# Sliding attention with 640-column key tiles and one 256-column product pair for every query tile

## Chip, cores and metric

The kernel runs on one core of one Trainium2 chip, as one launch. The metric is the device time of an execution in microseconds. Before the change the median of 3 runs is 2957.75 us (2957.2 to 2959.73).

## The reference, cut to what matters

Two transformer blocks over 2048 tokens of width 1024. The part that the change touches is the second block's mixer: causal attention in a window of 128 keys, 16 query heads in 4 groups, 4 key and value heads (one per group), head width 64, a bias by distance and a sink per head.

```python
def banded_attention(q, k, v, t5_table, window, sinks=None):
    ...
    kb = jnp.concatenate([kp[:, :, j:j + nb] for j in range(nprev + 1)], axis=3)
    ...
    s = jnp.einsum('bgrnqd,bgnkd->bgrnqk', qb, kb) * (Dh ** -0.5)
    ...
    s = jnp.where(valid, s + bias[None, :, :, None], NEG)
    ...
    o = jnp.einsum('bgrnqk,bgnkd->bgrnqd', p.astype(v.dtype), vb)
```

A tile of 128 queries needs 256 keys: its own 128 and the 128 in front of them. `xn @ w_in` gives q, k, v and a gate z; the output is `(o * silu(z)) @ w_out`, added to the residual and normalised.

## The kernel before, in words

`kernel_body` runs stages one after the other: projections of the first block (`phase_a`), its two attentions (`phase_b1`, `phase_b2`), its output and gate (`phase_c`), the sliding attention with its projections (`phase_d`), and the last product (`phase_e`). Every value that goes into a product is kept as a high and a low half, so a projection is three products for each k (`mm3`, lines 803 to 806). Tensors pass between stages through DRAM.

`phase_c` ends, for each tile t of 128 tokens, with `part3(t)` (lines 916 to 927): it scales the row tile `c_xt` by the norm and by `c_ng` (line 922), transposes it in eight 128-column pieces (line 839, out `c_tp`), and stores both halves to `s_xt`, 512 tokens to a tensor. `part2(15)` and `part3(15)` are the last work of the stage.

`phase_d` takes the tokens in 4 blocks of 512. `load_x` (line 1015) loads eight `e_x` tiles of 512 KB for a block from `s_xt`; each projection (q, z, v, k; output in `e_mm`, three PSUM buffers) walks over k = 0 to 7 of them. `kproj` writes four pairs of key tiles `kst` of 512 columns (`e_k`, one pair per group, high and low); before it writes a block's keys it copies the last 128 columns of the block before to `kpv` (`e_kp`, line 1061, on POOL). `scores(n)` handles step n = 16·block + 4·group + j, one tile of 128 queries and one group: for each of 4 heads it makes 128x256 scores in `e_s`. For j > 0 that is one pair of products with 256 columns (high and low key half, line 1106). For j = 0 the keys lie in two tiles, and it is a pair with 128 columns on `kpv` (line 1110) and another on `kst` (line 1112). DVE adds the bias and takes the maximum (line 1114), ACT the exponential, POOL the scaling; `values(n)` follows two steps later: eight transposes (line 1141), the split on ACT and DVE (lines 1145, 1146), four products of 512 columns (lines 1150, 1151), the sum on DVE (line 1158), the gate on POOL and a store. The projections of the next group or block are dealt out between the steps as pieces (lines 1164 to 1201).

`phase_e` (lines 1207 to 1270) loads and splits the weights into `f_w`, and for each tile t splits `f_yr` into `f_y` (ACT line 1239, then POOL line 1240), runs 48 products (`f_mm`), adds the tile `f_xt` (line 1252 loads it) and normalises.

The order of instructions on each engine and on SP's queue is made at build time by a planner, which takes what is ready by its own simulation, in program order among the ready ones; on the chip each queue then runs in that order.

**Where tiles lie.** A stage's pools are stacked in the order in which they are opened, from the same start, in bytes per partition; the next stage's pools are laid over them once the stage is closed. A pool of the next stage that lies over an old pool waits for the old one. Worked out from the tile shapes, the pools that matter are:

| stage c | bytes | stage d | bytes | stage e | bytes |
|---|---|---|---|---|---|
| c_a (`c_at`) | 40960 to 65536 | e_p | 64512 to 76800 | f_x1 (7 `f_xt`) | 53248 to 81920 |
| c_x (3 `c_xt`) | 65536 to 77824 | e_kv (`e_kp`) | 76800 to 80896 | f_s | 81920 to 83200 |
| c_wo1 (weights) | 77824 to 110592 | e_s | 80896 to 81664 | f_w1 | 83200 to 115968 |
| c_y1 | 110592 to 114688 | e_a0 (8 `e_x`) | 81664 to 114432 | f_y (2 `f_y`) | 115968 to 132352 |
| c_t, c_s | 114688 to 124352 | e_a1 (5 `e_x`) | 114432 to 134912 | f_j | 132352 to 134400 |
| c_w (`c_wg`, `c_wj`, `c_ng`) | from 124352 | e_q (8 `e_q`) | 134912 to 151296 | f_x2 (2 `f_xt`) | 134400 to 142592 |
| | | e_z, e_v | 151296 to 175872 | | |
| | | e_k (`e_k`) | 175872 to 192256 | | |

The 13 `e_x` buffers are used in turn: block 0 has the eight of e_a0, block 1 starts with the five of e_a1, and block 3 has its k = 0 and 1 in e_a1 and k = 2 to 7 in e_a0.

Of the kernel before, what the change touches and what calls it, by code (L numbers as in the profile page):

```python
# [7 lines left out]
F32 = mybir.dt.float32  # L8
F32R = mybir.dt.float32r
# [7 lines left out]
P = 128  # L17
# [963 lines left out]
def phase_d(tc, c, scr, a_w_in):  # L981
    nc = tc.nc
# [3 lines left out]
    with (  # L986
# [3 lines left out]
        tc.tile_pool(name="e_b", bufs=2) as bp,  # L990
        tc.tile_pool(name="e_t", bufs=2) as tp,
        tc.tile_pool(name="e_p", bufs=3) as pp,
        tc.tile_pool(name="e_kv", bufs=1) as kvp,
        tc.tile_pool(name="e_s", bufs=6) as sp,
        tc.tile_pool(name="e_a0", bufs=8) as ap0,
        tc.tile_pool(name="e_a1", bufs=5) as ap1,
# [8 lines left out]
        tc.tile_pool(name="e_po", bufs=1, space=PSUM) as ps_o,  # L1005
    ):
        toep = scr["toep"].rearrange("h r u -> h (r u)")[:, 127:127 + P * 383].rearrange("h (p w) -> p h w", w=383)
        kst = [[kp.tile([P, 512], F32R, name=f"e_k{g}{i}") for i in range(2)] for g in range(4)]
        kpv = [[kvp.tile([P, P], F32R, name=f"e_kp{g}{i}") for i in range(2)] for g in range(4)]
        vts, xts, qs, zs, units, bias, st = {}, {}, {}, {}, {}, {}, {}  # L1010

        def load_x(blk):
# [17 lines left out]
        def tmode(blk, key, m):  # L1030
            ps = pm.tile([P, 512], F32, name="e_mm")
            ms = slice(m * P, (m + 1) * P)
            for k in range(KD):
                w = units[key][k // 4]
                x = xts[blk, k]
                mm3(nc, ps, w[:, 0, k % 4, ms], w[:, 1, k % 4, ms], x[:, 0], x[:, 1], k == 0, k == KD - 1)
            return ps
# [17 lines left out]
        def kproj(blk, m):  # L1055
            ps = tmode(blk, ("k", blk), m)
            for e in range(2):
                g = 2 * m + e
                if blk > 0:
                    for i in range(2):  # L1060
                        nc.gpsimd.tensor_scalar(kpv[g][i], kst[g][i][:, 384:512].bitcast(F32), 1.0, 1.0,
                                                ALU.mult, ALU.mult)
                src = ps[64 * e:64 * e + 64]
                kh, kl = kst[g]
                for half in range(2):
                    hs = slice(64 * half, 64 * half + 64)
                    nc.scalar.activation(kh[hs], src, AF.Copy)
                    nc.vector.tensor_sub(kl[hs], src, kh[hs].bitcast(F32))  # L1068
# [15 lines left out]
        def scores(n):  # L1084
            blk, g, j = n // 16, (n // 4) % 4, n % 4
            t = blk * BT + j
            first = t == 0
            c0 = 128 if first else 0
            qsl = slice(j * P, (j + 1) * P)
            if j == 0:  # L1090
                b = bp.tile([P, 4, 256], F32, name="e_bias")
                nc.sync.dma_start(b, toep[:, 4 * g:4 * g + 4, 0:256])
                bias[blk, g] = b
            b = bias[blk, g]
            es = ep.tile([P, 4, 256], F32, name="e_es")
            mx = sp.tile([P, 4], F32, name="e_mx")
            ll = sp.tile([P, 4], F32, name="e_l")
            kk = kst[g]
            for r in range(4):
                if r % 2 == 0:  # L1100
                    ps2 = ps_s.tile([P, 2, 256], F32, name="e_s")
                ps = ps2[:, r % 2]
                q = qs[blk, g, r]
                if j > 0:
                    for i in range(2):
                        nc.tensor.matmul(ps, q[:, qsl], kk[i][:, (j - 1) * P:(j + 1) * P], start=i == 0, stop=i == 1)  # L1106
                else:
                    if not first:
                        for i in range(2):
                            nc.tensor.matmul(ps[:, 0:P], q[:, qsl], kpv[g][i], start=i == 0, stop=i == 1)  # L1110
                    for i in range(2):
                        nc.tensor.matmul(ps[:, P:256], q[:, qsl], kk[i][:, 0:P], start=i == 0, stop=i == 1)
                hd = 4 * g + r
                nc.vector.tensor_tensor_reduce(es[:, r, c0:], ps[:, c0:], b[:, r, c0:], 1.0, sk8[:, hd:hd + 1],  # L1114
                                               ALU.add, ALU.max, mx[:, r:r + 1])
            nm = sp.tile([P, 4], F32, name="e_nm")
            nc.vector.tensor_scalar(nm, mx, -0.125, None, ALU.mult)
            for r in range(4):
                nc.scalar.activation(es[:, r, c0:], es[:, r, c0:], AF.Exp, bias=nm[:, r:r + 1], scale=0.125,
                                     accum_out=ll[:, r:r + 1])  # L1120
            sk = sp.tile([P, 4], F32, name="e_sk4")
            nc.vector.tensor_sub(sk, sk8[:, 4 * g:4 * g + 4], mx)
            nc.scalar.activation(sk, sk, AF.Exp, scale=0.125)
            nc.vector.tensor_add(ll, ll, sk)
            nc.vector.reciprocal(ll, ll)  # L1125
            for r in range(4):
                nc.gpsimd.tensor_scalar(es[:, r, c0:], es[:, r, c0:], ll[:, r:r + 1], 0.5, ALU.mult, ALU.mult)  # L1127
            st[n] = es
# [43 lines left out]
        def block_pieces(blk):  # L1172
            yield lambda: load_x(blk)
            yield from group_pieces(blk, 0)
            yield lambda: load_unit(("v", blk), 1280)
            for j in range(BT):
                yield lambda j=j: vproj(blk, j)
            yield lambda: load_unit(("k", blk), 1024)
            for m in range(2):
                yield lambda m=m: kproj(blk, m)  # L1180
# [6 lines left out]
        for n in range(N + LAG):  # L1187
            blk, g, j = n // 16, (n // 4) % 4, n % 4
            if n < N and j == 0:
                nxt = group_pieces(blk, g + 1) if g < 3 else block_pieces(blk + 1) if blk + 1 < NB else iter(())  # L1190
                pend = list(nxt)
                per = -(-len(pend) // 4)
            if n < N:
                scores(n)
            for f in pend[:per // 2]:
                f()
            if n >= LAG:
                values(n - LAG)
            for f in pend[per // 2:per]:
                f()  # L1200
            pend = pend[per:]
# [126 lines left out]
def kernel_body(tc, a, out):  # L1328
    with (
        tc.tile_pool(name="const", bufs=1) as cp,  # L1330
        tc.tile_pool(name="dram", bufs=1, space=DRAM) as dp,
    ):
        c = consts(tc, cp)
        scr = make_scratch(dp)
        phase_a(tc, c, a["x"], a["w_in"], a["mix_norm_g"],
                [a["diff_q_norm_g"], a["diff_k_norm_g"], a["dil_q_norm_g"], a["dil_k_norm_g"]], scr,
                lambda pm: [
                    diff_lambda(tc, c, [a["lambda_q1"], a["lambda_k1"], a["lambda_q2"], a["lambda_k2"]]),
                    prep_swa(tc, c, scr, a["t5_table_2"], a["t_onehot"], a["a_sinks_2"], pm)])
        phase_b1(tc, c, scr, a["t_ndist"], a["diff_sub_norm_g"], c["lam"])  # L1340
        phase_b2(tc, c, scr, a["t_nat"], a["t_res"], a["t_two"])
        phase_c(tc, c, scr, a["x"], a["p"], a["w_out"], a["ple_norm_g"], a["w_ple_gate"], a["w_ple_proj"],
                a["norm_g_2"])
        phase_d(tc, c, scr, a["a_w_in_2"])
        phase_e(tc, c, scr, a["a_w_out_2"], a["final_g_2"], out)
# [29 lines left out]
```

## Time and profile before

| | |
|---|---|
| median of 3 runs | 2957.75 us |
| the profiled execution | 2958.66 us |
| its span in the trace | 2956.9 us |
| instructions | 45164 |
| PE, weight loads, DVE, ACT, POOL busy | 97%, 83%, 61%, 53%, 42% |

The profiled execution is 0.91 us above the median, and 1.76 us of it lie around the span. In rows of instructions the first number is the start in us from the span's start, the second the time that the row covers, then the engine (PEld is the weight load, SPq the DMA issue on SP), the line, the operation, out<-in, the shape and the count. A matmul's own duration contains its way through the array, so that what it costs in a stream is read from the distance of the starts.

### The profile page before, as it was taken

The numbers are of one execution on the slowest core, as the hardware profiler recorded it, in microseconds if no ns is written. First come the engines' busy times: TensorE is split into PE (matmuls) and PEld (weight loads), VectorE is DVE, ScalarE is ACT, GpSimd is POOL, SyncE is SP. The second block draws the span as 40 slices with busy tenths as digits, with TensorE's granted clock in tenths as the row PEclk, the third lists the DMA queues.
The fourth block names the chain that finished last, engine by engine and source line by source line (L and its number), as shares of the span: only waits on it lengthen the run. The fifth ranks groups of instructions, "written<-read, shape, count | busy, mean of one in ns | idle before, by whom it ended". The sixth has DMA issues, their size and how long they took to land.

```text
span 2956.9 us, 45164 instructions
## 1 busy us (share of the span) xinstructions
PE 2878.8 (97%) x15554; PEld 2455.2 (83%) x15554; DVE 1803.7 (61%) x4607; ACT 1562.5 (53%) x3480; POOL 1239.1 (42%) x1156
## 2 busy tenths in 40 slices
PE   9999999999999999989999899999999999999998
PEld 7878888888798888878999778888788888888787
DVE  4215556522688888887877654444535756666855
ACT  5222333221588888878989442222345756665621
POOL 1110111001488888864777700000156555555421
PEclk9999999999999999999999899999999999999999
DMA  6663444424314132129786633232554243332552
GB/s 208 116 160 86 122 114 121 96 87 115 121 30 115 46 106 65 51 64 189 143 164 133 180 116 110 77 113 92 183 166 155 86 157 96 109 100 72 156 182 79
DMA packets 410646, 346.00 MB, mean 117 GB/s; under 512 B 89745, under 2 KB 356401, under 8 KB 408497
## 3 DMA queue, kind: packets, MB, share of 16 engines
q1 hardware_dynamic: 388000, 329.24, 40.2%
q10 hardware_dynamic: 20736, 8.65, 1.8%
q0 software_dynamic: 1680, 5.21, 0.7%
q8 instruction: 124, 2.03, 0.3%
q14 instruction: 106, 0.86, 0.1%
HBM read 227.51 MB, written 116.52 MB: 116 GB/s over the span
## 4 chain that ended last, share of the span: by engine, by line
PE 86%; DMA 5%; DVE 3%; ACT 2%; SPq 1%; issue 1%; POOL 0%; DVEq 0%; ACTq 0%; POOLq 0%
PE s_ps L331 8%; PE psm L190 7%; PE psm L192 7%; PE psm L191 7%; PE e_mm L804 5%; PE e_mm L806 5%; PE e_mm L805 5%; PE c_mm L804 4%; PE c_mm L805 4%; PE c_mm L806 4%; PE t_ps L375 3%; PE o_ps L389 2%; PE o_ps L391 2%; PE o_ps L390 2%; PE d_sr L590 2%; PE f_mm L805 2%
## 5 line engine op out<-in xcount | busy, mean ns | idle before, releaser
L190 PE MATMUL psm<-w,hh 128*128 128x512 f32 x1024 | 406.3, 398 | 9.4 <-DVE t L111 8.0
L191 PE MATMUL psm<-w,hl 128*128 128x512 f32 x1024 | 399.5, 391 | 0.0
L192 PE MATMUL psm<-w,hh 128*128 128x512 f32 x1024 | 399.5, 393 | 0.0
L101 POOL TENSOR_TENSOR w<-wraw,w 128x512 fp32r<-128x512 f32 x64 | 81.5, 1294 | 600.2 <-ACT w L100 589.9
L365 POOL TENSOR_TENSOR et<-et 128x1024 f32<-128x1024 f32 x124 | 296.0, 2409 | 0.0
L331 PE MATMUL s_ps<-kst,qst 128*128 128x512 f32 x1024 | 289.7, 407 | 5.5 <-DVE mx L337 3.7
L347 ACT ACTIVATE et<-et,nm 128x2048 f32<-128x2048 f32 x128 | 257.2, 2009 | 5.2
L1026 POOL TENSOR_TENSOR e_wt<-e_raw,e_wt 128x1024 fp32r<-128x1024 f32 x80 | 191.3, 2399 | 111.9 <-ACT e_wt L1025 110.9
L190 PEld LDWEIGHTS psm<-w,hh 128*128 128x128 f32 x1024 | 193.5, 189 | 48.3 <-DVE t L111 8.4
L804 PE MATMUL e_mm<-e_x,e_wt 128*128 128x512 f32 x576 | 228.2, 396 | 1.2 <-DVE e_k L1068 0.8
L806 PE MATMUL e_mm<-e_x,e_wt 128*128 128x512 f32 x576 | 226.8, 394 | 0.0
L192 PEld LDWEIGHTS psm<-w,hh 128*128 128x128 f32 x1024 | 192.9, 189 | 40.9
L805 PE MATMUL e_mm<-e_x,e_wt 128*128 128x512 f32 x576 | 226.6, 393 | 0.0
L191 PEld LDWEIGHTS psm<-w,hl 128*128 128x128 f32 x1024 | 193.7, 189 | 38.2
L331 PEld LDWEIGHTS s_ps<-kst,qst 128*128 128x128 f32 x1024 | 175.9, 190 | 45.3 <-DVE mx L337 18.1
L1127 POOL TENSOR_SCALAR e_es<-e_es,e_l 128x256 f32<-128x256 f32 (+1 forms) x256 | 119.4, 485 | 170.8 <-DVE e_l L1125 118.6
L364 POOL TENSOR_SCALAR et<-et,cc 128x1024 f32<-128x1024 f32 x124 | 138.2, 1129 | 110.3 <-PE psm L192 57.1
L377 DVE TENSOR_TENSOR ptl<-t_ps,pth 128x512 fp32r<-128x512 f32 x256 | 169.4, 684 | 19.9 <-ACT pth L376 16.8
L337 DVE CUSTOM_DVE_ANT_0 et<-s_ps,nd,mx 128x1024 f32<-128x1024 f32 x128 | 163.9, 1280 | 26.5 <-PE s_ps L331 24.7
L1114 DVE CUSTOM_DVE_ANT_0 e_es<-e_s,e_bias,e_sk 128x256 f32<-128x256 f32 (+1 forms) x256 | 117.4, 473 | 102.6 <-PE e_s L1106 71.2
L376 ACT ACTIVATE pth<-t_ps 128x512 fp32r<-128x512 f32 x256 | 143.6, 595 | 44.8 <-PE t_ps L375 41.1
L850 POOL TENSOR_TENSOR c_yn<-c_yn,ssq_sub 128x512 f32<-128x512 f32 x16 | 17.0, 1061 | 354.1 <-DMA c_yn<-s_y 354.1
(268 smaller groups left out, 7848.2 us busy)
## 6 DMA issues: line engine op xcount, KB each, us to landing
e_raw<-in_a_w_in_dram SPq DMA_DIRECT2D x80, 512.0 KB, 3.7
wraw<-in_w_in_dram SPq DMA_DIRECT2D x64, 256.0 KB, 3.5
kst<-s_dk SPq DMA_DIRECT2D x128, 128.0 KB, 4.2
s_xt<-c_at SPq DMA_DIRECT2D x32, 512.0 KB, 6.8
e_x<-s_xt SPq DMA_DIRECT2D x32, 512.0 KB, 7.1
t<-in_x_dram SPq DMA_DIRECT2D x32, 256.0 KB, 5.4
s_dv<-t SPq DMA_DIRECT2D x32, 256.0 KB, 3.3
s_bv<-t SPq DMA_DIRECT2D x32, 256.0 KB, 3.6
```

The source lines that it names most:

```text
L190: nc.tensor.matmul(ps, ah, cur[k][:, 0], start=k == 0, stop=False)
L191: nc.tensor.matmul(ps, al, cur[k][:, 0], start=False, stop=False)
L192: nc.tensor.matmul(ps, ah, cur[k][:, 1], start=False, stop=k == KD - 1)
L331: nc.tensor.matmul(ps[:, b * 512:b * 512 + 512], lhs, heads[h, "k", e, i, 2 * hf + b], start=i == 0, stop=i == 1)
L337: nc.vector.tensor_tensor_reduce(et[:, hf], ps, bias[:, off:off + 1024], 1.0, -3.0e38 if hf == 0 else mx[:, 0:1], ALU.add, ALU.max, mx[:, ...
L347: nc.scalar.activation(ev, ev, AF.Exp, bias=nm, scale=slope, accum_out=st[g]["l"][:, e:e + 1])
L365: nc.gpsimd.tensor_sub(es[0][:, hf], es[0][:, hf], es[1][:, hf])
L377: nc.vector.tensor_sub(tl[:, :, qi], pt, th[:, :, qi].bitcast(F32))
L804: nc.tensor.matmul(ps, ah, bh, start=first, stop=False)
L805: nc.tensor.matmul(ps, al, bh, start=False, stop=False)
L806: nc.tensor.matmul(ps, ah, bl, start=False, stop=last)
L1026: nc.gpsimd.tensor_sub(w[:, 1], raw, w[:, 0].bitcast(F32))
```

## The change

The pool e_kv with the `e_kp` tiles goes. The key tiles have 640 columns: 128 for the keys in front of the block, then the block's 512. The POOL copy goes into the first 128 columns of the same tile, and every query tile is scored by one pair of products with 256 columns (128 for the first tile of all). The instruction count falls by 96 products with their weight loads. In the stack of stage d the pools e_s to e_v begin 4096 bytes earlier (e_s at 76800, e_a0 at 77568, e_a1 at 110336, e_q at 130816), e_k begins at 171776 and ends at 192256 as before.

```diff
-        tc.tile_pool(name="e_kv", bufs=1) as kvp,
...
-        kst = [[kp.tile([P, 512], F32R, name=f"e_k{g}{i}") for i in range(2)] for g in range(4)]
-        kpv = [[kvp.tile([P, P], F32R, name=f"e_kp{g}{i}") for i in range(2)] for g in range(4)]
+        kst = [[kp.tile([P, P + 512], F32R, name=f"e_k{g}{i}") for i in range(2)] for g in range(4)]
...
-                        nc.gpsimd.tensor_scalar(kpv[g][i], kst[g][i][:, 384:512].bitcast(F32), 1.0, 1.0,
+                        nc.gpsimd.tensor_scalar(kst[g][i][:, 0:P], kst[g][i][:, 512:].bitcast(F32), 1.0, 1.0,
                                                 ALU.mult, ALU.mult)
...
-                kh, kl = kst[g]
+                kh, kl = [k[:, P:] for k in kst[g]]
...
-                if j > 0:
-                    for i in range(2):
-                        nc.tensor.matmul(ps, q[:, qsl], kk[i][:, (j - 1) * P:(j + 1) * P], start=i == 0, stop=i == 1)
-                else:
-                    if not first:
-                        for i in range(2):
-                            nc.tensor.matmul(ps[:, 0:P], q[:, qsl], kpv[g][i], start=i == 0, stop=i == 1)
-                    for i in range(2):
-                        nc.tensor.matmul(ps[:, P:256], q[:, qsl], kk[i][:, 0:P], start=i == 0, stop=i == 1)
+                for i in range(2):
+                    nc.tensor.matmul(ps[:, c0:], q[:, qsl], kk[i][:, j * P + c0:(j + 2) * P], start=i == 0, stop=i == 1)
```

## Rows read from the trace of the kernel before

**Rows 1.** The page, busy time of each engine over the span.
```profile
PE 2878.8 (97%) x15554; PEld 2455.2 (83%) x15554; DVE 1803.7 (61%) x4607; ACT 1562.5 (53%) x3480; POOL 1239.1 (42%) x1156
```

**Rows 2.** Busy time by stretch: one block of stage d.
```profile
core 0: us, PE busy (x) PEld busy (x) DVE busy (x) ACT busy (x) POOL busy (x), PEclk, DMA share, GB/s
2335.00:2491.00 156.00, 156.00 (x868) 134.71 (x867) 96.22 (x287) 98.63 (x247) 92.76 (x125) 1.00 0.39 122
```

**Rows 3.** The instructions of line 1110: min/median/max ns, first and last start.
```profile
L1110 PE MATMUL e_s<-e_kp,e_q x96: 220/274/307, 2332.4 to 2762.6; 128*128 128x128 f32 x96
```

**Rows 4.** PE in order of time, 2728.3 to 2730.2: one head at j = 0.
```profile
2728.30 0.40 PE L804 MATMUL e_mm<-e_x,e_wt 128*128 128x512 f32 x1
...
2728.99 0.33 PE L1110 MATMUL e_s<-e_kp,e_q 128*128 128x128 f32 x2
2729.16 0.39 PE L1112 MATMUL e_s<-e_k,e_q 128*128 128x128 f32 x2
...
2730.13 0.39 PE L804 MATMUL e_mm<-e_x,e_wt 128*128 128x512 f32 x1
```

**Rows 5.** PE in order of time, 2737.8 to 2739.5: one head at j > 0.
```profile
2737.85 0.40 PE L804 MATMUL e_mm<-e_x,e_wt 128*128 128x512 f32 x1
...
2738.55 0.40 PE L1106 MATMUL e_s<-e_k,e_q 128*128 128x256 f32 x2
...
2739.48 0.39 PE L804 MATMUL e_mm<-e_x,e_wt 128*128 128x512 f32 x1
```

**Rows 6.** All engines at 2106: c_wo's last product, block 0's first load.
```profile
2105.99 0.40 PE L806 MATMUL c_mm<-c_wo,c_at 128*128 128x512 f32 x1
...
2106.42 0.34 SPq L1015 DMA_DIRECT2D e_x<-s_xt  x1
```

**Rows 7.** DVE, then SP's queue, at 2144: c_ng's last use, block 1's loads.
```profile
2143.11 1.28 DVE L922 SCALAR_TENSOR_TENSOR c_xt<-c_xt,rd_y,c_ng 128x1024 f32<-128x1024 f32 x1
...
2144.53 3.37 SPq L1015 DMA_DIRECT2D e_x<-s_xt  x5
```

**Rows 8.** All engines at 2791: the last scores, two loads of f_xt.
```profile
2790.91 0.40 PE L1106 MATMUL e_s<-e_k,e_q 128*128 128x256 f32 x2
...
2791.68 0.95 SPq L1252 DMA_DIRECT2D f_xt<-s_x  x2
```

**Rows 9.** PE at 2138: transposes of part3(14), first projection of stage d.
```profile
2137.86 1.03 PE L839 MATMUL c_tp<-id,c_xt 128*128 128x128 f32 x8
2138.87 0.50 PE L804 MATMUL e_mm<-e_x,e_wt 128*128 128x512 f32 x1
```

**Rows 10.** Line 1015 in 2144 to 2148: issues, and issue to landing.
```profile
L1015 SPq DMA_DIRECT2D e_x<-s_xt x5: 332/443/1539, 2144.5 to 2147.5; - x5
...
DMA to landing us min/median/max: 4.7/6.4/7.2
```

**Rows 11.** PE idle before 2750.20, and by stretch the 4.8 us behind it.
```profile
2750.20 0.91 PE L1106 MATMUL e_s<-e_k,e_q 128*128 128x256 f32 x4 [2.76 <-DVE e_mx L1114]
...
2750.20:2755.00 4.80, 4.75 (x21) 3.90 (x21) 4.73 (x18) 4.75 (x17) 2.12 (x5) 0.64 0.81 263
```

**Rows 12.** By stretch, 2755.66 to 2791.30: all instructions, then those of f_mm alone.
```profile
2755.66:2791.30 35.64, 34.85 (x183) 28.59 (x183) 29.04 (x85) 25.76 (x66) 19.69 (x32) 1.00 0.38 110
...
2755.66:2791.30 35.64, 25.50 (x96) 17.11 (x96) 1.51 (x3) 1.00 0.38 110
```

**Rows 13.** Groups by line in the same stretch: DVE's work for the steps.
```profile
L1114 DVE CUSTOM_DVE_ANT_0 e_es<-e_s,e_bias,e_sk 128x256 f32<-128x256 f32 x16 | 7.4, 475 | 0.4 <-PE e_s L1106 0.3
...
L1146 DVE TENSOR_TENSOR e_pl<-e_tp,e_ph 128x512 fp32r<-128x512 f32 x10 | 6.6, 684 | 0.1
...
L1158 DVE TENSOR_TENSOR e_o<-e_o,e_tmpb 64x256 f32<-64x256 f32 x10 | 4.1, 415 | 1.2 <-ACT e_tmpb L1153 1.1
```

**Rows 14.** Who writes f_y: min/median/max ns, first and last start.
```profile
L1239 ACT ACTIVATE f_y<-f_yr x16: 1043/1062/1064, 2745.7 to 2926.8; 128x1024 fp32r<-128x1024 f32 x16
L1240 POOL TENSOR_TENSOR f_y<-f_yr,f_y x16: 2354/2394/2402, 2746.8 to 2928.0; 128x1024 fp32r<-128x1024 f32 x16
```

## The prediction

> **What bounds the kernel now.** I read the page first: PE is busy for 97% of the span, and apart from its own weight loads nothing for more than 61% [rows 1]. Then the stage: in the block from 2335 to 2491 us PE is busy for all 156.00 us [rows 2], so there every product taken from PE shortens the kernel by what it costs in the stream. Then the two kinds of scores in the order of time [rows 4, 5], for that cost. Last the two seams, from `phase_c` to `phase_d` and from there to `phase_e`, since the change also moves pools, and a PE without work is paid in full where PE is the bound.
>
> **The saving: 8.8 us.** 96 instructions of line 1110 [rows 3] are two for each of 48 heads at j = 0 (3 blocks, 4 groups, 4 heads); each such head has two on line 1112 too, and makes two of 256 columns instead of four of 128. In [rows 4] 1.83 us pass from 2728.30 to 2730.13, with six products of 512 columns besides the four narrow ones (three before and three behind); in [rows 5] 1.63 us pass with six such products and the wide pair. The difference, 0.20 us, is a head's saving: 48 x 0.20 = 9.6 us. The last four heads (step 60) lie in the tail, where PE will not be the bound (below): 44 x 0.20 = 8.8 us. In parts: a 512-column product takes 0.23 us (2737.85 to 2738.55 holds three), so the wide pair costs 1.63 - 1.38 = 0.25 us and the four narrow ones 0.45, 0.11 each against 0.125. The Trainium skill (TensorE: Matmul & The Clock Gate, Back-to-back issue gap) lists for an isolated product 134 cycles at 128 columns and 262 at 256, warm; by that four narrow ones would cost as much as two wide ones and the saving would be nil. The measured rows decide.
>
> **The copy: nothing.** Same size, same engine, two for each group and block. It is now a write to the tile that the next block's keys are written to; those writes wait for the last scores of the group anyway. If the copy too waits for all scores on that tile, POOL stands a little longer, and `e_k` is late by a copy: under 1 us a block at worst, so 0 to 3 us. I take 0, PE having other projections there.
>
> **The first seam: e_a0 now lies over c_x, 15 us.** Pools wait whole. Block 0's first `e_x` load is issued at 2106.42, as the last product on `c_wo` (2105.99) ends [rows 6], though its own bytes lie under the weights of k = 0 and 1. Block 1's loads go at 2144.53, just after line 922 has read `c_ng` for the last time (2144.39), though `c_ng` lies behind their own bytes: they share a pool's edge, not bytes [rows 7]. The third case is at the other seam: `f_xt` for t = 2 goes 0.4 us after the last scores, the last reader of `e_q` [rows 8]. With e_a0 at 77568 and c_x up to 77824, 256 bytes overlap, and block 0's eight loads wait no longer for the weights but for the last `c_xt`, that of `part3(15)`. Line 922 ends at 2144.39, its eight transposes take 1.03 us [rows 9], so the loads go at about 2145.4 instead of 2106.42. PE has no other work: today it starts the projections at 2138.87 [rows 9], and all of them need block 0's `e_x`.
>
> How long: from issue to landing takes 4.7 us for the first tile, and the five of block 1, issued in 3.0 us, land 1.3 us apart [rows 10]. If block 0's go first, x of k = 0 lands at 2150.1, PE idles from 2138.9 less the 1.03 of transposes that it has to do anyway: 10 us. If block 1's five (ready 1 us earlier, with SP idle) go first, 5 x 1.3 us come on top: 16 us. I take 13, about half of them in front. Behind it, one projection wants a tile every 0.69 us (three products) and gets one every 1.3 us: 7 x 0.6 = 4 us, or 0 where the two others with a free PSUM buffer run beside it; I take 0, as the planner takes what is ready. And the clock: after PE had been idle for 2.76 us, the granted clock was 0.64 over the next 4.8 us [rows 11], between its levels of 2.4 and 1.2 GHz; that costs 4.8 x 0.36 = 1.7 us. Together 15 us, from 10 to 22.
>
> **The second seam: f_y now lies over e_q, 11 us.** f_y ends at 132352; e_q began at 134912 and now begins at 130816. Today `f_y` is first written at 2745.7 [rows 14], and tiles 0 and 1 of `phase_e` fill PE while the last steps 60 to 63 wait for DVE, ACT and POOL: 96 products of `f_mm`, 96 x 0.23 = 22 us of the 35.64 us up to the last scores [rows 12]. After the change `f_y` waits for the last scores. So the last steps run alone. How fast: DVE has for them 4 x 4 x 0.475 us for the scores and 3 x (2 x 0.684 + 2 x 0.415) us for the values in front, 7.6 + 6.6 = 14 us if nothing else ran on it; with all that it does in this stretch it is busy for 29 us [rows 12, 13]. I take 20 us, nearer to the first, since the steps come first in program order; the weight splits of `phase_e` stay and share DVE and ACT. Then ACT's 1.06 us before the first `f_mm`, and 2.39 us on POOL before the first product with the low half [rows 14], which the remaining values partly cover. In these 21 us PE does 15 heads x 0.25 us and four steps of values at 8 x 0.11 + 4 x 0.23 = 1.8 us: 11 us; idle are 10, and with the slower clock 1 more. Bounds: 14 us of steps with three values leave 14 + 1 - 9 = 6 us; 29 us leave 30 - 11 = 19.
>
> **The sum.** -8.8 + 15 + 11 = +17.2 us against the profiled execution's 2958.66, so 2975.9; the median lies 0.9 lower: **2975.0 us**. Bounds: -8.8 + 10 + 6 = +7, and -8.8 + 22 + 19 + 3 = +35.
>
> **Rivals.**
> *Faster: the pools' shift costs nothing.* Either a load waits only for tiles still in use under its own bytes (seven of block 0's eight then wait for nothing new, and the projections can start on what is there), or the planner finds an order that hides both waits. Then the saving stands alone: 2957.75 - 9.6 = 2948.1 us. It decides at the point where the first load of block 0 goes before about 2134 (4.7 us ahead of 2138.87). Against it stand three places where the whole pool is waited for [rows 6 to 8]. Chance 0.09.
> *Only the first seam:* the tail is long enough on other engines that `f_mm` is not missed, or `f_y` comes early. 2957.75 - 8.8 + 15 = 2964. Chance 0.12.
> *Only the second:* block 0's loads are not held. 2957.75 - 8.8 + 11 = 2960, no change that can be told. Chance 0.06.
> *Narrow products are not dear.* If a product cost by its columns alone, with 0.23 us for 512, four of 128 would cost as much as two of 256 and nothing would be saved: 2957.75 + 26 = 2984. The skill's list above would have it so. Rows 4 and 5 speak against it; chance 0.03.
> That the products are the same sums, only joined, is plain from the diff; no rival there.
>
> **How the numbers follow.** A measurement of this kernel tells 0.2%, 5.9 us, from no change: from 2951.8 to 2963.7. The forecast has 0.70. Slower is the forecast, narrow products, and half of the first-seam case, whose time is at the edge: 0.70 + 0.03 + 0.06 = 0.79. Same is the other half and the second-seam case, 0.12; faster is the first rival, 0.09. The range goes from 2959, which takes in either seam alone, to 2986, +28, short of the upper bound +35, which needs every cost at its worst; it leaves out the faster rival and that end.
>
> **What would show it.** Right: no line 1110, and 512 instructions of 256 or (first block) 128 columns on the one line of scores; block 0's `e_x` loads issued after 2144, a PE gap of about 10 us behind the transposes of `part3(14)` whose releaser is a DMA, granted clock below 1 behind it; `f_y` first written after the last scores, no `f_mm` before them, and PE idle for some 10 us between. Wrong: the first `e_x` load near 2106, or `f_mm` among the last scores, while blocks of stage d take about 3 us less each; then the time is below 2957. If both gaps are there and the sum is off, it is the number of block 1's loads in front, or the pace of the last four steps, that I sized wrong.

## The result, and the profile after

| | median, us | kernel before beside it, us | ratio, with its interval |
|---|---|---|---|
| the changed kernel | 2980.96 (2980.44 to 2985.84) | 2958.74 | 1.0077 [1.0059, 1.0094] |
| the same again | 2984.59 | 2958.46 | 1.0090 [1.0071, 1.0109] |

The change costs 22.2 us; the forecast was 17.2. In the second row one slow run of the kernel before, 3546.79 us at a granted clock of 0.75, is left out. The profiled execution took 2980.67 us, with a span of 2978.9 us.

In the rows PE is the engine of the matrix products (TensorE), DVE is VectorE, ACT ScalarE, POOL GpSimd, and SP issues the DMA transfers. The page of the changed kernel, the span and the busy time of each engine, against [rows 1]:

```profile
span 2978.9 us, 44985 instructions
PE 2879.9 (97%) x15458; PEld 2450.7 (82%) x15458; DVE 1805.5 (61%) x4607; ACT 1561.8 (52%) x3480; POOL 1240.0 (42%) x1156
```

PE has 96 products fewer than in [rows 1], the other engines' totals are within 5 us of those there, and still the span is 22.0 us longer. So no engine got more work worth speaking of: the time is in waits of PE and in its clock. The products themselves came out as the diff says, one line of scores in place of three:

```profile
L1103 PE MATMUL e_s<-e_k,e_q x512: 220/282/580, 2203.1 to 2787.4; 128*128 128x256 f32 x160, 128*128 128x128 f32 x11
```

Inside the stage PE is as full as in [rows 2]. By stretch, 160 us of the changed kernel's stage d (columns as in [rows 2]):

```profile
2320.00:2480.00 160.00, 160.00 (x886) 137.72 (x886) 106.48 (x309) 104.50 (x261) 95.73 (x133) 1.00 0.38 123
```

So the loss is at the ends of the stage. **The first seam**: PE in order of time, against [rows 9], then SP's queue over the same stretch, against [rows 6, 7, 10].

```profile
2135.81 0.39 PE L806 MATMUL c_mm<-c_wj,c_pT 128*128 128x512 f32 x1
2136.04 1.03 PE L839 MATMUL c_tp<-id,c_xt 128*128 128x128 f32 x8
2142.71 1.94 PE L839 MATMUL c_tp<-id,c_xt 128*128 128x128 f32 x8 [5.64 <-DVE c_xt L922]
2154.19 0.76 PE L804 MATMUL e_mm<-e_x,e_wt 128*128 128x512 f32 x1 [9.54 <-DMA e_x<-s_xt]
```

```profile
2142.71 2.94 SPq L1013 DMA_DIRECT2D e_x<-s_xt  x6
...
2146.31 3.75 SPq L1013 DMA_DIRECT2D e_x<-s_xt  x1
...
2150.62 6.17 SPq L1013 DMA_DIRECT2D e_x<-s_xt  x6
```

Before, PE went from one set of transposes straight to the projections. Now it waits 5.64 us for the last `c_xt` of phase_c, makes its transposes, and waits 9.54 us for a DMA of `e_x`. No `e_x` load goes before 2142.71, where block 0's first one went at 2106.42. Six go in a row there. Five, those of block 1, go as line 922 ends (2142.57). The sixth, at 2145.11, goes behind the last transposes (2144.65) and is block 0's k = 0, the one that PE wants: its landing at 2154.05 ends PE's wait. Seven more follow from 2146.31. Behind the gap, by stretch:

```profile
2136.20:2154.19 17.99, 2.82 (x16) 2.23 (x15) 7.22 (x18) 3.00 (x6) 0.00 (x0) 0.60 0.86 291
2154.19:2159.00 4.81, 4.81 (x15) 3.88 (x16) 0.00 (x0) 0.54 (x1) 0.00 (x0) 0.70 1.07 395
2159.00:2180.00 21.00, 19.27 (x86) 15.49 (x85) 3.44 (x5) 6.80 (x10) 8.94 (x4) 1.00 0.66 235
```

PE is busy for 2.82 of 17.99 us; then the granted clock is 0.70 for 4.81 us, between its two levels of 1.2 and 2.4 GHz, and only then 1.00. The missing 1.73 us of the third line is one more wait, the last in the next view, PE's waits from 2080 to 2800 (columns: who waited, for whom, us in total, times, longest):

```profile
PE e_mm L804 <- DMA e_x<-s_xt: 9.5, 1, 9.5
PE c_tp L839 <- DVE c_xt L922: 5.6, 1, 5.6
...
PE e_mm L804 <- DVE e_z L1050: 1.7, 1, 1.7
```

**The second seam**: PE in order of time, then ACT's first `f_y`, then by stretch, from the last `e_mm` to the four last steps (the last 32 products of `e_s`, four heads and eight products to a step) and from there to the first `f_mm`, against [rows 12, 14].

```profile
2754.52 0.39 PE L806 MATMUL e_mm<-e_x,e_wt 128*128 128x512 f32 x1
...
2767.77 1.01 PE L1103 MATMUL e_s<-e_k,e_q 128*128 128x256 f32 x4
...
2787.05 0.78 PE L1103 MATMUL e_s<-e_k,e_q 128*128 128x256 f32 x2
...
2788.98 0.72 PE L804 MATMUL f_mm<-f_w,f_y 128*128 128x512 f32 x2
...
2970.57 0.28 PE L806 MATMUL f_mm<-f_w,f_y 128*128 128x256 f32 x1
```

```profile
L1230 ACT ACTIVATE f_y<-f_yr x16: 1058/1062/1064, 2787.9 to 2948.9; 128x1024 fp32r<-128x1024 f32 x16
```

```profile
2754.91:2767.77 12.86, 9.13 (x43) 6.93 (x41) 10.33 (x36) 9.30 (x27) 4.41 (x8) 0.74 0.59 188
2767.77:2788.98 21.21, 16.53 (x83) 12.05 (x81) 20.15 (x74) 19.95 (x57) 11.44 (x24) 0.91 0.38 109
```

`f_y` is first written at 2787.9, as the last scores end, and the first `f_mm` starts at 2788.98; before it was there at 2755.66, 36 us ahead of the last scores. Without it PE is idle for 3.7 us of the first stretch and 4.7 us of the second, at a clock of 0.74 and 0.91, where [rows 12] have 34.85 of 35.64 us busy at 1.00. In the second stretch DVE is busy for 20.15 of 21.21 us.

**Where the time went.** Stage d begins some us earlier or later from one execution to the next (the last `c_mm` ends between 2134 and 2145 us), whatever was changed in it. So I compare lengths between three ends: of the last `c_mm`, the last `e_mm` and the last `f_mm`. From before, PE in order of time at the three:

```profile
2137.63 0.40 PE L806 MATMUL c_mm<-c_wj,c_pT 128*128 128x512 f32 x1
...
2746.58 0.40 PE L806 MATMUL e_mm<-e_x,e_wt 128*128 128x512 f32 x1
...
2948.55 0.28 PE L806 MATMUL f_mm<-f_w,f_y 128*128 128x256 f32 x1
```

| kernel | last c_mm to last e_mm | last e_mm to last f_mm | first e_mm after last c_mm |
|---|---|---|---|
| before | 608.9 | 201.9 | +0.8 |
| after | 618.7 | 215.9 | +18.0 |
| after, again | 618.8 | 217.4 | +17.2 |

Between the ends the changed kernel is 9.8 + 14.0 = 23.8 us longer; up to the first of them it was 1.8 us ahead, which leaves the span's 22.0. The saving is hidden in the 9.8.

The ends don't cut the two kernels alike. All products of `e_s` behind the last `e_mm`, with DVE's work on them (one instruction a head), before and after (PE, PEld and DVE only):

```profile
2746.75:2950.00 203.25, 10.01 (x54) 8.52 (x54) 10.66 (x23) 0.99 0.43 144
...
2754.70:2972.00 217.30, 13.25 (x52) 9.48 (x52) 12.23 (x26) 0.98 0.41 136
```

Behind that end the kernel before has 23 heads, 56 transposes and 32 products of values left, the changed one 26, 64 and 33. At the prediction's prices that is 3 x 0.25 + 8 x 0.11 + 0.23 = 1.9 us of work that moved from the first length to the second. Where products are joined, all kernels below have the changed kernel's counts; the kernel of experiment 2, with the old products, has those of before. Only lengths with like counts can be subtracted without this correction.

### The profile page after: what moved, and what is told of

Its sections match the earlier page's. It is cut to its first block, busy times and chain, and to the rows that moved or that the text cites. A ratio compares the mean times of both kernels' runs of the same rounds, so it can differ in the third digit from the quotient of the medians.

```text
span 2978.9 us, 44985 instructions
## 1 busy us (share of the span) xinstructions
PE 2879.9 (97%) x15458; PEld 2450.7 (82%) x15458; DVE 1805.5 (61%) x4607; ACT 1561.8 (52%) x3480; POOL 1240.0 (42%) x1156
## 4 chain that ended last, share of the span: by engine, by line
PE 86%; DMA 5%; DVE 3%; ACT 3%; SPq 1%; issue 1%; POOL 1%; DVEq 0%; ACTq 0%; POOLq 0%
PE s_ps L331 7%; PE psm L190 7%; PE psm L192 7%; PE psm L191 7%; PE e_mm L804 5%; PE e_mm L805 5%; PE e_mm L806 5%; PE c_mm L804 4%; PE c_mm L805 4%; PE c_mm L806 4%; PE t_ps L375 3%; PE f_mm L805 2%; PE o_ps L389 2%; PE f_mm L806 2%; PE f_mm L804 2%; PE o_ps L391 2%
```

## The experiments

Where no other is named, edits are to the changed kernel. Theory A is the prediction's: three independent terms, a saving and two seams made by where the pools lie. The rivals: the products' shape, the copy or the joined tile cost time themselves; the first seam is only the order of loads.

**1. The products without the shift.** Two of `e_z`'s five buffers go into the place where `e_kv` stood, so that the pools from `e_s` to `e_z` begin where they began before; products, copy and tiles are the change's.

```
+        tc.tile_pool(name="e_z0", bufs=2) as zp0,
         tc.tile_pool(name="e_s", bufs=6) as sp,
-        tc.tile_pool(name="e_z", bufs=5) as zp,
+        tc.tile_pool(name="e_z", bufs=3) as zp,
-            z = zp.tile([P, 512], F32, name="e_z")
+            z = (zp0 if len(zs) % 5 < 2 else zp).tile([P, 512], F32, name="e_z")
```

> The change with its joined products, but two of the five e_z buffers stand where e_kv stood, so that e_s to e_q lie at the bytes of before. Layout theory: both seams go back to what they were (first load of block 0 near 2106, f_mm among the last scores) and only the saving of 48 heads x 0.20 us is left: 9.6 us below the kernel before, about 2949 us. Rival (the loss comes from the joined products or from the copy into the key tile, within the blocks): the time stays near the changed kernel, 2975 to 2981 us.

Measured: 0.9973 [0.9963, 0.9983], and on another chip 0.9977 [0.9968, 0.9986]: faster than before by some 7 us. PE and SP's queue in order of time:

```profile
2111.89 0.34 SPq L1014 DMA_DIRECT2D e_x<-s_xt  x1
...
2143.09 0.39 PE L806 MATMUL c_mm<-c_wj,c_pT 128*128 128x512 f32 x1
...
2742.89 0.39 PE L806 MATMUL e_mm<-e_x,e_wt 128*128 128x512 f32 x1
...
2948.18 0.28 PE L806 MATMUL f_mm<-f_w,f_y 128*128 128x256 f32 x1
```

Block 0's first load goes 31 us ahead of the last `c_mm` again, and 98 products of `f_mm` go ahead of the last scores. From the last `c_mm` to the last `e_mm` are 599.8 us (599.2 in the second run) against 608.9: 9.1 us less, of which 1.9 is the moved work, so **the saving up to there is 7.2 us**. PE is idle for 2.2 us of this length, 1.7 before. So products, copy and joined tile cost nothing that shows, and the changed kernel's loss is in the layout. From the last `e_mm` to the last `f_mm` are 205.2 us, 3.3 more than before: the moved work, a little more idle PE and a clock of 0.93 over the 47 us up to the last scores, 0.96 before. Why the last steps fell that way here stays open. Over both lengths the kernel is 5.8 us shorter.

**2. The shift without the products.** In the kernel before, only the pool `e_kv` moves from in front of `e_s` to behind `e_k`, so that `e_a0` lies at 77568 and `e_q` at 130816, as in the change.

```
-        tc.tile_pool(name="e_kv", bufs=1) as kvp,
         tc.tile_pool(name="e_s", bufs=6) as sp,
...
+        tc.tile_pool(name="e_kv", bufs=1) as kvp,
```

> The kernel before with its narrow products and its e_kp tiles, but the pool e_kv opened behind e_k: the bytes of the change without its products. Layout theory: the seams' cost alone, 22 us measured plus the 9 us saved that hid in it, so 31 us above the kernel before, about 2990 us. Rival (products or copy are to blame): no change, about 2959 us.

Measured: 1.0104 [1.0090, 1.0117], 30.8 us at 2966.05 us for the kernel before beside it, with the same products, copies and tiles. PE in order of time:

```profile
2149.59 1.94 PE L839 MATMUL c_tp<-id,c_xt 128*128 128x128 f32 x8 [5.64 <-DVE c_xt L922]
...
2160.86 0.77 PE L804 MATMUL e_mm<-e_x,e_wt 128*128 128x512 f32 x1 [9.33 <-DMA e_x<-s_xt]
```

The same two waits to a tenth of a microsecond, but for 9.33 instead of 9.54. Its lengths are 630.1 and 212.9 us, 21.2 and 11.0 above before, with the same counts. The move of one pool of 4096 bytes a partition makes both seams by itself.

**3. The second seam alone.** Four more buffers of `e_s` (512 bytes) lift `e_a0` off `c_x`, to 78080; `f_y` still lies over `e_q`.

```
-        tc.tile_pool(name="e_s", bufs=6) as sp,
+        tc.tile_pool(name="e_s", bufs=10) as sp,
```

> The change with four more small buffers in e_s, 512 bytes, so that e_a0 begins at 78080, behind c_x, while e_q (131328) still lies under f_y. Layout theory: the first seam is gone (15 to 17 us), the second stays: 2964 to 2966 us, first e_x of block 0 near 2105, no f_mm before the last scores. Rival (256 bytes of overlap can't hold eight 4096-byte tiles, the loss has another place): no change from 2981 us.

Measured: 1.0027 [1.0018, 1.0036]. The first `e_mm` starts 0.8 us after the last `c_mm`, as before, the length from there is 599.7 us as in experiment 1, and **512 bytes take the whole first seam away**. Its tail (last `e_mm` to last `f_mm`) is worse than the changed kernel's: 222.9 us, 17.7 above experiment 1's. By stretch, to the first `f_mm` and from there to the last:

```profile
2737.65:2775.70 38.05, 28.27 (x125) 21.54 (x125) 34.27 (x116) 31.60 (x89) 17.03 (x33) 0.78 0.50 150
2775.70:2960.58 184.88, 182.09 (x818) 151.19 (x816) 99.73 (x226) 43.61 (x96) 45.77 (x31) 0.97 0.38 129
```

PE idles for 9.8 us at a clock of 0.78, and the clock stays below 1.00 behind it. The clock's share is at most 0.22 x 38.05 + 0.03 x 184.88 = 13.9 us, in the changed kernel 0.26 x 12.86 + 0.09 x 21.21 = 5.2: more than the 7.0 us between the two tails. That the added buffers, which the small tiles of the scores use too, played no part is not shown. By ratios, the second seam is 1.0027 - 0.9975 = 0.52%, 15 us (0.9975 is the mean of experiment 1's two ratios), and the first is what is left to the changed kernel: 1.0084 (the mean of its four ratios, those of experiment 6 with them) - 1.0027 = 0.57%, 17 us, each good to some 4 us by the intervals.

**4. The order of loads.** Block 0's first five tiles take `e_a1`, whose place comes free first, and the others `e_a0`; the pools lie as in the change.

```
-                x = (ap0 if len(xts) % 13 < 8 else ap1).tile(...)
+                x = (ap1 if len(xts) % 13 < 5 else ap0).tile(...)
```

> The change with the 13 e_x buffers taken from e_a1 first, so that block 0's k = 0 to 4 wait for c_w (free about 1 us earlier than c_x) and no load of block 1 stands in front of them. If the five loads in front (1.3 us each) make up part of the first seam, the first projection starts 6 us earlier and the time is about 2975 us. If the seam is all waiting for c_x and transfer, no change from 2981 us.

Measured: 1.0054 [1.0038, 1.0070]. PE in order of time:

```profile
2147.51 1.94 PE L839 MATMUL c_tp<-id,c_xt 128*128 128x128 f32 x8 [5.64 <-DVE c_xt L922]
...
2151.41 0.76 PE L804 MATMUL e_mm<-e_x,e_wt 128*128 128x512 f32 x1 [1.96 <-DMA e_x<-s_xt]
```

The wait for the DMA falls from 9.54 to 1.96 us, the length from 618.7 to 611.8 us. So 7 us of the first seam are block 1's five loads in front, at the 1.3 us apart of [rows 10]: 5 x 1.3 = 6.5. The 5.64 us stay, and the order alone is not the seam.

**5. What a narrow product costs.** In experiment 1's kernel every score outside block 0's first tile is made in four products of 128 columns.

```
-                for i in range(2):
-                    nc.tensor.matmul(ps[:, c0:], q[:, qsl], kk[i][:, j * P + c0:(j + 2) * P], start=i == 0, stop=i == 1)
+                for a in range(c0, 256, P):
+                    for i in range(2):
+                        nc.tensor.matmul(ps[:, a:a + P], q[:, qsl], kk[i][:, j * P + a:j * P + a + P], start=i == 0, stop=i == 1)
```

> The refilled layout of e1, but every query tile scored in products of 128 columns: 240 heads take four narrow products instead of a wide pair, where the kernel before has 48. If a narrow product costs nearly what a wide one costs (0.20 us a head, as rows 4 and 5 have it), 192 more heads than before, 12 of them in the tail: 180 x 0.20 = 36 us above the kernel before, ratio about 1.012. If products cost by their columns, the ratio is that of e1, 0.997.

Measured: 1.0140 [1.0122, 1.0158]. PE in order of time:

```profile
2142.49 0.39 PE L806 MATMUL c_mm<-c_wj,c_pT 128*128 128x512 f32 x1
...
2785.91 0.39 PE L806 MATMUL e_mm<-e_x,e_wt 128*128 128x512 f32 x1
```

That is a length of 643.4 us, 34.5 above the kernel before. The two have nearly the same counts behind the last `e_mm` (24 heads here, 23 there; transposes and values alike). Up to it 216 heads take four narrow products here and 44 there: 34.5 / 172 = 0.20 us a head, as in [rows 4, 5]. The same columns in twice as many products cost that much more. The list of the Trainium skill (TensorE: Matmul & The Clock Gate, Back-to-back issue gap), which is for isolated products and by which four narrow ones cost as much as two wide ones, does not hold for this stream. In it every product comes with a weight load of its own (PE and PEld both x15458 in the changed kernel).

**6. Waiting by tile.** A pool's option for waits by tile was set on `e_a0`, `f_y` and `f_j`, then on the last two alone (one of the two edits):

```
-        tc.tile_pool(name="e_a0", bufs=8) as ap0,
+        tc.tile_pool(name="e_a0", bufs=8, reuse_waits="tile") as ap0,
```

> The changed kernel with its layout as it is, but e_a0, f_y and f_j wait only for the tiles under their own bytes and not for whole pools. Layout theory: the second seam goes (16 us by e1 and e3). At the first, k = 0 of block 0 waits for the third c_xt (tile 14, its transposes end just before the first projection starts) and lands 4 to 5 us later; the other seven are early: the seam shrinks from 15 to about 4 us. Together 8 - 4 = 4 us below the kernel before, ratio 0.9985. Rival (the bytes matter and not the pool): no change from 1.0077.

> As e6, but f_y and f_j alone wait by tiles; e_a0 waits for the whole of c_x as in the change. Layout theory: the second seam alone goes: 1.0077 less 16 us (0.0054) = 1.0023. If the two seams are not separate (the tail being idle anyway), it stays near 1.0077.

Measured: 1.0085 [1.0069, 1.0101] and 1.0082 [1.0066, 1.0098], no change, against the layout theory's expectation. But the order of instructions on every engine is that of the changed kernel, so the option brought nothing forward, and whether pools or bytes are waited for is not decided by it. The two serve as two more runs of the changed kernel. Whether the whole pool is waited for was then asked with smaller pools.

**7. A smaller pool at each seam.** At the first, `e_a0` becomes a pool of one buffer over `c_x`'s end, taken by block 0's k = 7, and a pool of seven behind it; no buffer moves.

```
-        tc.tile_pool(name="e_a0", bufs=8) as ap0,
+        tc.tile_pool(name="e_a00", bufs=1) as ap00,
+        tc.tile_pool(name="e_a0", bufs=7) as ap0,
-                x = (ap0 if len(xts) % 13 < 8 else ap1).tile(...)
+                x = (ap0 if len(xts) % 13 < 7 else ap00 if len(xts) % 13 == 7 else ap1).tile(...)
```

> The changed kernel with every tile at the same bytes, but e_a0 opened as two pools: one buffer at 77568 (over c_x), which holds k = 7 of block 0, and seven from 81664 on, clear of c_x. Layout theory: only k = 7 waits for c_x; k = 0 to 6 of three projections (63 products, 14 us) cover its way, and the first seam all but goes: 1.0084 (mean of the four measurements of the changed program) less 0.005 = 1.0034. Rival (the 256 bytes are no matter, the loads are late for another reason): no change from 1.0084.

Measured: 1.0053 [1.0034, 1.0072]. SP's queue, and then PE, in order of time:

```profile
2111.29 0.34 SPq L1014 DMA_DIRECT2D e_x<-s_xt  x1
2112.16 2.85 SPq L1014 DMA_DIRECT2D e_x<-s_xt  x6
...
2151.70 3.05 SPq L1014 DMA_DIRECT2D e_x<-s_xt  x5
...
2157.92 0.45 SPq L1014 DMA_DIRECT2D e_x<-s_xt  x1
```

```profile
2164.25 0.47 PE L804 MATMUL e_mm<-e_x,e_wt 128*128 128x512 f32 x1 [2.71 <-DMA e_x<-s_xt]
```

Seven loads go early again, and only the one that shares the 256 bytes is held, behind block 1's five. The length is 605.0 us: of the seam's 18.9 us (618.7 - 599.8) **13.7 come back without one buffer moved**, where 15 were expected; by the ratios it is 1.0084 - 1.0053 = 0.31%, 9 us, with intervals of some 6 us. The held tile still costs the 2.71 us of the last row. This settles that a load waits for its whole pool: seven buffers that share no byte with `c_x` wait when they are one pool with the eighth, and don't when they are not. The tail, 216.9 us, keeps the second seam.

At the second seam `f_y` becomes two pools of one buffer, of which only the second lies over `e_q`.

```
-        tc.tile_pool(name="f_y", bufs=2) as yp,
+        tc.tile_pool(name="f_y", bufs=1) as yp0,
+        tc.tile_pool(name="f_y1", bufs=1) as yp1,
-            y = yp.tile([P, 2, KD, P], F32R, name="f_y")
+            y = (yp0, yp1)[t % 2].tile([P, 2, KD, P], F32R, name="f_y")
```

> The changed kernel with every tile at the same bytes, but the two f_y buffers opened as two pools: the first ends at 124160, before e_q, the second lies over e_q. Layout theory: tile 0's 48 products (11 us) fill the tail again, tile 1's 48 don't: 11 of the second seam's 16 us come back, 1.0084 less 0.0037 = 1.0047, with f_mm before the last scores. Rival (the tail is idle for want of scores and values, not for want of f_mm): no change from 1.0084.

Measured: 1.0067 [1.0048, 1.0087]. By stretch, 2762.80 to 2801.00, the last scores' end: everything, then `f_mm` alone (PE, PEld and DVE only).

```profile
2762.80:2801.00 38.20, 31.77 (x159) 24.83 (x159) 32.62 (x107) 29.91 (x85) 18.68 (x32) 0.91 0.49 150
...
2762.80:2801.00 38.20, 14.24 (x42) 7.65 (x42) 0.68 (x1) 0.91 0.49 150
```

One tile of `phase_e`, 42 products, is back among the last steps, where [rows 12] have 96, and the last length is 210.3 us, 5.6 less than the changed kernel's 215.9. Four traces of the changed program have 215.5 to 217.4 there, so the step is plain by the rows; by time alone it is small (the two intervals overlap). The 11 us expected were too many: of the 10.7 us by which the changed kernel's tail is above experiment 1's, one of two tiles gives back about half.

**8. The best version, another way.** `e_v` in place of `e_z` fills the gap: two of its seven buffers.

```
+        tc.tile_pool(name="e_v0", bufs=2) as vp0,
-        tc.tile_pool(name="e_v", bufs=7) as vp,
+        tc.tile_pool(name="e_v", bufs=5) as vp,
-            vt = vp.tile([P, 4, 2, 64], F32R, name="e_vt")
+            vt = (vp0 if len(vts) % 7 < 2 else vp).tile([P, 4, 2, 64], F32R, name="e_vt")
```

> The refilled kernel of e1 once more, on another chip: 0.9973 before, 8 to 9 us below the kernel before.

> As e1, but two of the seven e_vt buffers stand where e_kv stood; e_s to e_z lie at the bytes of before. If it is the bytes of e_a0 and e_q that count and not what fills the gap, the time is that of e1 within 0.1%: ratio 0.997. If the refill with e_z has a cost or gain of its own (e1's tail is 3 us longer than that of the kernel before), the two differ.

Measured: 0.9977 [0.9968, 0.9986] and 0.9976 [0.9967, 0.9984] on one chip, no difference. Both beat the kernel before, by 7 us, and the change as it stands by some 30. It doesn't matter which pool fills the gap, so long as the pools from `e_s` to `e_q` stay where they were.

## Why the prediction was right, and where its sizes were off

The forecast of slower, by two seams that outweigh a saving, held; both seams and the saving were shown apart.

| term | forecast, us | measured, us | the same on the other way, us |
|---|---|---|---|
| saving, both lengths | -8.8 | -5.8 (before to experiment 1) | -8.4 (experiment 2 to the change) |
| copy | 0 | nothing that shows | nothing that shows |
| first seam | +15 | +18.9 = 618.7 - 599.8 | +21.2 = 630.1 - 608.9 |
| second seam | +11 | +10.7 = 215.9 - 205.2 | +11.0 = 212.9 - 201.9 |
| sum | +17.2 | +23.8 | +23.8 |

The four kernels make a square, old or joined products with old or shifted pools, and there are two ways from before to the change: products first (by experiment 1) or pools first (by experiment 2). Each seam is taken between kernels with like counts behind the last `e_mm`. The 23.8 us between the ends are 22.2 in the runs. On the first way the forecast is 6.6 us short: 3.9 in the first seam, 3.0 in the saving, less 0.3 in the second seam.

*The saving* had the right price, and so the choice of measured rows over a price by columns was right: experiment 5 shows 0.20 us a head. But only 5.8 to 8.4 us of 8.8 arrive, 7 by the ratios of experiments 1 and 8, and up to the last `e_mm` 7.2 for 44 heads. Part of what is missing is the longer tail of experiment 1; the rest stays open.

*The first seam* had the right mechanism, the loads' issue behind `c_xt` instead of at 2106.42, and was sized 4 to 6 us too low. This is the term that was off most. "About half of them in front" was the choice between a gap of 10 and one of 16 us; all five of block 1 went in front, and PE was idle for 5.64 + 9.54 = 15.2 us, where I took 13. Experiment 4 shows these five to be worth 7 us. Behind the gap, where I took 0, 1.7 us turned up as one wait for `e_z`. The clock cost 0.9 us in the transposes (1.94 for 1.03) and 0.30 x 4.81 = 1.4 behind the gap, 2.3 against 1.7. Together 15.2 + 1.7 + 2.3 = 19.2, against the 18.9 measured.

*The second seam* also had the right mechanism and, between kernels with like counts, the right size. "I take 20 us" for the four steps came true: their first scores start at 2767.77 and the last end at 2787.83, 20.1 us (21.0 in the second run of the change). The shares differ from the forecast's, 10 idle and 1 for the clock. In the 21.21 us up to the first `f_mm` PE idles for 4.7 us, and a clock of 0.91 takes up to 1.9. PE counts as busy for 16.53 us, where the forecast has 11 us of work; I take the difference for products that run singly and slowly, which is not shown. What the forecast did not see is the stretch before, 10 heads that were left when the projections ran out. It is idle for 3.7 us at a clock of 0.74, but it is as idle where there is no seam, in experiment 1:

```profile
2743.28:2759.66 16.38, 12.50 (x62) 10.36 (x61) 12.52 (x37) 12.38 (x31) 9.29 (x10) 0.79 0.65 198
```

The tail is not the same in all kernels that have the seam: against experiment 1 it is 10.7 us longer in the change, 11.7 in experiment 7's first kernel, and 17.7 in experiment 3, where the granted clock was lower (0.78 over 38.05 us). What sets the clock's course there I can't resolve further.

*The rivals.* "Faster: the pools' shift costs nothing" fell with the first load at 2142.71, and experiment 7 shows why: whole pools are waited for, and where the pool is cut, most of the seam goes. "Only the first" and "only the second" fell with the rows of both seams; experiment 3 is the second alone, and slower by 0.27%, which I had put within the noise. "Narrow products are not dear" fell with experiments 1 and 5.

## What to carry to other kernels

Where pools of successive stages are laid over each other, a pool that is removed moves all behind it, and 256 bytes of new overlap can make a stage's first loads wait for the end of the stage before: list what each first tile newly overlaps before counting what an edit saves. If a gap opens, fill it with buffers of another pool, or cut the pool that touches the old one so that one buffer waits and not all. Ask also which loads become ready at the same moment, and give the place that comes free first to the tile that is wanted first.

## What the runs showed of the hardware

The clock's price came in more places than the gap itself. The eight transposes behind 5.64 us of idle took 1.94 us, the eight in front of it 1.03; by stretch, both:

```profile
2142.71:2144.65 1.94, 1.94 (x8) 1.54 (x8) 0.18 (x1) 0.60 (x1) 0.00 (x0) 0.50 0.93 243
2136.04:2137.07 1.03, 1.03 (x9) 0.79 (x7) 0.73 (x2) 0.40 (x1) 0.00 (x0) 1.00 0.00 0
```

The granted clock is 0.50, the lower level, in the one and 1.00 in the other. The first projections behind 9.54 us ran at 0.70 for 4.81 us. More surprising was the tail: no wait of PE there is over 2.4 us, and yet the granted clock was 0.74 over 12.86 and 0.91 over 21.21 us. In experiment 3, with no wait over 2.9 us, it was 0.78 over 38.05 us. So many short waits of PE can cost more than half as much again in clock as in idle time (at most 5.2 beside 8.4 us, and 0.22 x 38.05 = 8.4 beside 9.8).
